# A retention head's values and normalised rows, transposed by DMA as two planes of 16-bit halves

## The chip, the cores and the metric

The kernel runs on one core of one Trainium2 chip. The time is device microseconds of one execution, the median of several runs; a profiled execution gives the trace. The engines are called as in the profile: PE (TensorE, its weight loads as PEld), DVE (VectorE), ACT (ScalarE), POOL (GpSimd), and SP, whose queue issues every DMA of this kernel.

## The reference

One layer of a decoder trunk: RMS norm, one input projection, two kinds of mixer side by side, an output projection, a residual and a last RMS norm. Sequence 2,048 (and 16 learned meta tokens ahead of it), width 1,024, all in float32.

```python
proj = einsum('bld,de->ble', rms_norm(h), w_in)          # 1024 -> 8 x 512
cx, cb, cc, cg, q, k, v, rg = split(proj, 8)
conv_out = short_conv(cx, cb, cc, conv_w) * silu(cg)     # 4 groups of 128
qf, kf = rotary(q) * 128**-0.5, rotary(k)                # 4 heads of 128
ret = retention_chunkwise(qf, kf, v)                     # chunks of 128, decay per head
y = (ret - mean(ret)) * rsqrt(var(ret) + eps)            # per head and row
ret_out = y * ret_norm_g * silu(rg)
out = rms_norm(h + concat(conv_out, ret_out) @ w_out) * final_g
```

Retention by chunks: `scores = (q k^T) * decay`, `out = scores v + q state`, and `state = decay * state + (k * zeta)^T v` from chunk to chunk.

## The kernel before

**Layout.** Sequence positions are handled in two halves of 1,024 (`r` = 0, 1; `NR`), each in two blocks of 512 columns (`j` = 0, 1; `HB`), each of four chunks of 128 (`c`; `CH`). A projection is computed with the 128 features of a head or group on the partitions and 512 positions in the free dimension.

**Quads.** Projections and the output projection are products of 2 x 2 blocks. `quad` (L203) does a 2 x 2 by 2 x 2 block product with seven products in place of eight (a Strassen-Winograd form), each product being 12 matmuls of 128 x 128 by 128 x 512: four slices of the contraction, with each operand split into a rounded high part and a low rest, and three of the four cross products. The line of all these matmuls is L212. A block's high part is made by a cast on ACT (`wh`, L101) and the rest by a subtraction on DVE (`wl`, L113). Both go through rings of three tiles (`RING`), so that ACT and DVE run at most three products ahead of PE. Sums of weight blocks are made on POOL (L110, L113) in raw tiles (`ra`, eight of them, `RAW`). Three times in a quad a PSUM bank is copied to SBUF by ACT (`copy`, L219), after the products numbered 0, 2 and 3. The function `take` handles each of the four results as it is done. `quad_plain` is the plain form with eight products, used at the start of each half.

**Units.** A half has eight units, in the order of `UNITS`: four `conv_group`s and four `head`s (in the first half a convolution group comes first, then heads 0 to 3; in the second, heads 0 to 3 and then the groups). A unit has two quads. Head `h` projects keys and values in the first quad and queries and gate in the second; `take` adds the bank copy to the bank (or copies the bank by ACT where there is nothing to add, L585), turns queries and keys (`rotary`), and applies SiLU to the gate (`sg`). Then, for each block `j`:

- four PE transposes of the keys (L631), scaled by `kd_col` on ACT (L633); four PE transposes of the values (L636), each chunk scaled by its rows' factors on ACT (L640, out of PSUM into the same tile);
- the chunks' state products (L646) and the chain of states (L649);
- scores (L659), masked and scaled (L661); output `o` from scores and state (L669, L670);
- mean and variance of each row (L675, L677), the power on POOL (L682), the normalised rows `y` on DVE (L686), in the tile `pm`;
- four PE transposes of `y` into a PSUM bank (L693); one DVE instruction multiplies this by the norm gain and the gate (L694); `store_mixed` (L444) writes the result to a DRAM tensor `mixed`, which the output projection reads at the end.

Between heads of the first half, `prepare` loads blocks of x (L361), makes their block sums on DVE and stores them (L190) for the second half; in the second half the same is done for the output weights.

**What sets the order.** The kernel is written as straight program text; a planner at build time simulates the engines' timelines and fixes for each engine, and for SP's queue, one order of instructions. At run time each engine works through its list in order and waits at an instruction until its inputs and buffers are there. So the retention of one head is laid between the next head's quads on PE. `tc.issue_after(ins)` puts the instructions in its block behind `ins` in the list of `ins`'s engine, and binds no other engine. Most working tiles (`kv`, `qg`, `x`, `t`, `w`, and so on) come from one pool of 16 tiles (`gen`, tag `g`, `GEN` = 16). SP issues, in its order, weight loads (L436), x loads, stores of sums and `mixed` stores.

Of the kernel before, what the change touches and what calls it, by code (L numbers as in the profile page):

```python
# [8 lines left out]
F32 = mybir.dt.float32  # L9
F32R = mybir.dt.float32r  # L10
BF16 = mybir.dt.bfloat16
AF = mybir.ActivationFunctionType
ALU = mybir.AluOpType

P = 128
# [6 lines left out]
HB = 512  # L22
NR = 2
BLK = SEQ // NR
CH = HB // P
KH = KT // 2
# [44 lines left out]
def hybrid_trunk(ctx: ExitStack, tc: tile.TileContext, t, out: bass.AP, chunk_decay):  # L71
# [5 lines left out]
    nc = tc.nc  # L77
# [11 lines left out]
    def ps_misc():  # L89
        return ps.tile([P, HB], F32, name="ms", tag="ms", bufs=4)  # L90

    def gen(name="g"):
        return sb.tile([P, HB + 16], F32, name=name, tag="g", bufs=GEN)[:, : 2 + HB]
# [29 lines left out]
    def stationary(blocks):  # L123

        a11, a12, a21, a22 = blocks
        s1 = sb.tile([P, HB], F32, name="sa", tag="ra", bufs=RAW)

        def parts(src):
            hi = sb.tile([P, HB], F32R, name="wh", tag="wh", bufs=RING)
            lo = sb.tile([P, HB], F32R, name="wl", tag="wl", bufs=RING)  # L130
            split(hi, lo, src)
            return hi, lo

        w = [parts(a11), parts(a12)]
        add(nc.gpsimd, s1, a21, a22)
        sub(nc.gpsimd, a21, a11, a21)
        sub(nc.gpsimd, a11, s1, a11)
        sub(nc.gpsimd, a12, a12, a11)
        return w + [parts(a) for a in (a11, s1, a21, a12, a22)]
# [53 lines left out]
    def prepared(m, src, ns, held={}):  # L193

        for n in ns:
            for kt in range(KH):
# [3 lines left out]
                    nc.sync.dma_start(a, src[n, kt])  # L200
                parts(m, SUMS[n], kt, a)

    def quad(w, m, take):  # L203


        def product(i, bank, first):
            (wh, wl) = w[i]
            for kt in range(KH):
                ks = slice(kt * P, (kt + 1) * P)
                mh, ml = m[i][kt]  # L210
                for n, (a, b) in enumerate(((wl, mh), (wh, ml), (wh, mh))):
                    nc.tensor.matmul(  # L212
                        bank, a[:, ks], b, start=first and kt == 0 and n == 0, stop=kt == KH - 1 and n == 2,
                        skip_group_check=not first,
                    )

        def copy(bank):
            c = sb.tile([P, HB], F32, name="tc", tag="tc", bufs=COPIES)
            nc.scalar.copy(out=c, in_=bank)  # L219
            return c  # L220

        xb = ps_proj()
        product(0, xb, True)
        c = copy(xb)
        yb = ps_proj()
        product(1, yb, True)
        take(0, 0, yb, c)
        product(2, xb, False)
        u2 = copy(xb)
        zb = ps_proj()  # L230
        product(3, zb, True)
        c = copy(zb)
        product(4, xb, False)
        take(1, 1, xb, c)
        product(5, zb, False)
        take(0, 1, zb, u2)
        product(6, xb, False)
        take(1, 0, xb, None)
# [61 lines left out]
    ident = const.tile([P, P], F32, name="ident")  # L300
# [5 lines left out]
    ret_g = const.tile([P, NG], F32, name="ret_g")  # L306
# [135 lines left out]
    def store_mixed(r, j, kt, m):  # L442
        d = mixed[2 * r + j]
        nc.sync.dma_start(  # L444
            d[:, :, kt // KH, :, kt % KH, :].rearrange("a i p c -> p a i c"),
            m.rearrange("p (a i c) -> p a i c", a=2, i=2),
        )
# [67 lines left out]
    def conv_group(g, r, m, f, blocks, ahead):  # L515

        u = [gen("u") for _ in range(2)]
        rr, rr2 = ([a[:, j * HB : (j + 1) * HB] for j in range(2)] for a in f[:2])
        held = [None]

        def mul(eng, out, a, b):
            eng.tensor_tensor(out=out, in0=a, in1=b, op=ALU.mult)  # L522

        def take(i, j, pp, c):
            s = u[j][:, 2:]
            if c is None:
                mul(nc.vector, s, pp, s)
            elif i == 1:
                add(nc.vector, c, pp, c)
                held[0] = c  # L530
            else:
                add(nc.vector, s, pp, c)
                mul(nc.vector, s, s, rr2[j])
                if j == 1:
                    mul(nc.gpsimd, s, s, held[0])

        blocks, meta = blocks
        quad(stationary(blocks), m, take)
        if meta:
            meta_carry(g, meta)  # L540
        carry(u, g, r)
        cs = [taps(u[j], g) for j in range(2)]

        def take(i, j, pp, c):
            if i == 0:
                add(nc.vector, c, pp, c)
                mul(nc.vector, c, c, rr[j])
                nc.scalar.activation(c, c, AF.Silu)  # L548
                mul(nc.gpsimd, cs[j], cs[j], rr[j])
                mul(nc.gpsimd, cs[j], cs[j], c)  # L550
                return
            if c is not None:
                add(nc.vector, c, pp, c)
                pp = c
            mul(nc.vector, cs[j], pp, cs[j])

        n = 2 * (NG + g) + 1
        quad(stationary(load_raw(w_loads(n))), m, take)
        blocks = ahead()
        for j in range(2):  # L560
            store_mixed(r, j, g, cs[j])
        return blocks
# [3 lines left out]
    def rotary(a, table):  # L566
# [5 lines left out]
        nc.vector.tensor_tensor(out=a, in0=a, in1=table[:, 0, :], op=ALU.mult)  # L572
        turned[0] = nc.vector.tensor_tensor(out=a, in0=a, in1=rot[:, :w], op=ALU.add)

    def head(h, r, m, rot_t, f, blocks, ahead, first=(), between=()):


        between = iter(between)
        k, v = [None, None], [None, None]
        tables = [rot_t[:, :, j * HB : (j + 1) * HB] for j in range(2)]  # L580

        def take(i, j, pp, c):
            d = gen("kv")[:, :HB]
            if c is None:
                nc.scalar.copy(out=d, in_=pp)  # L585
            else:
                add(nc.vector, d, pp, c)
            if i == 0:
                rotary(d, tables[j])
                k[j] = d  # L590
            else:
                v[j] = d

        if len(first) > 0:
            quad_plain(first[0], m, take)
        else:
            quad(stationary(blocks[0]), m, take)
        next(between, lambda: None)()
        q, sg = [None, None], [None, None]

# [24 lines left out]
        blocks = ahead()  # L625
        states = [state[h]]
        vt = []
        for j in range(2):
            tp = ps_misc()
            for c in range(CH):  # L630
                nc.tensor.transpose(tp[:, c * P : (c + 1) * P], k[j][:, c * P : (c + 1) * P], ident)  # L631
            kd = brief("kd")
            nc.scalar.mul(kd, tp, kd_col[:, h : h + 1])  # L633
            tp = ps_misc()
            for c in range(CH):
                nc.tensor.transpose(tp[:, c * P : (c + 1) * P], v[j][:, c * P : (c + 1) * P], ident)  # L636
            vj = v[j]
            for c in range(CH):
                cs = slice(c * P, (c + 1) * P)
                nc.scalar.mul(vj[:, cs], tp[:, cs], f[2][j][0][:, c : c + 1])  # L640
            vt.append(vj)
            last = r == NR - 1 and j == 1
            up = ps_misc()
            for c in range(CH - last):
                cs = slice(c * P, (c + 1) * P)
                nc.tensor.matmul(up[:, cs], kd[:, cs], vj[:, cs], start=True, stop=True)  # L646
            for c in range(CH - last):
                nxt = sb.tile([P, P], F32, name="state", tag="state", bufs=2 * CH)
                nc.vector.scalar_tensor_tensor(  # L649
                    out=nxt, in0=states[-1], scalar=chunk_decay[h], in1=up[:, c * P : (c + 1) * P],  # L650
                    op0=ALU.mult, op1=ALU.add,
                )
                states.append(nxt)

        for j in range(2):
            sc = ps_misc()
            for c in range(CH):
                cs = slice(c * P, (c + 1) * P)
# [3 lines left out]
                out=pm.rearrange("p (c i) -> p c i", c=CH), in0=sc.rearrange("p (c i) -> p c i", c=CH),  # L662
                scalar=past_col[:, h : h + 1],
                in1=causal.rearrange("p (c i) -> p c i", c=1).broadcast_to([P, CH, P]), op0=ALU.mult, op1=ALU.mult,
            )
            o = ps_misc()
            for c in range(CH):
                cs = slice(c * P, (c + 1) * P)
# [14 lines left out]
            y = pm  # L683
            for c in range(CH):
                cs = slice(c * P, (c + 1) * P)
                nc.vector.tensor_scalar(  # L686
                    out=y[:, cs], in0=o[:, cs], scalar1=mv[:, c, 0:1], scalar2=rp[:, c, :],
                    op0=ALU.subtract, op1=ALU.mult,
                )
            yT = ps_misc()  # L690
            for c in range(CH):
                cs = slice(c * P, (c + 1) * P)
                nc.tensor.transpose(yT[:, cs], y[:, cs], ident)  # L693
            nc.vector.scalar_tensor_tensor(  # L694
                out=sg[j], in0=yT, scalar=ret_g[:, h : h + 1], in1=sg[j], op0=ALU.mult, op1=ALU.mult
            )
            store_mixed(r, j, KH + h, sg[j])
        if r < NR - 1:
            nc.gpsimd.tensor_copy(out=state[h], in_=states[-1])
        return blocks  # L700
# [81 lines left out]
    for r in range(NR):  # L782
        f = factors[r]
# [120 lines left out]
```

## Time and profile before

| | |
|---|---|
| median of 3 runs | 894.16 us (893.94 to 894.59) |
| the profiled execution | 893.76 us, its span 892.0 us |
| granted TensorE clock, mean | 0.999 |
| busy PE / DVE / ACT / POOL | 879.8 / 717.7 / 407.2 / 397.8 us |
| DMA | 116.94 MB, 131 GB/s mean |

Busy times are unions of an engine's instructions; a matmul's recorded length overlaps the next one's, so what an instruction occupies is read from the distance between starts. The heads of the first half lie between about 64 and 295 us, those of the second between about 389 and 606 us. In groups and timelines, `out<-in` are the program's tile names, and `L212` is a line of the kernel.

### The profile page before, as it was taken

Reading aid. Unit: us, or ns where it says so; the run is one execution under the profiler, and the core shown is the slowest. Engines: PE = TensorE matmul, PEld = TensorE weight load, DVE = VectorE, ACT = ScalarE, POOL = GpSimd, SP = SyncE. Lnnn points to the kernel's source line nnn. Section 1 sums busy time; section 2 is a strip of 40 time slices with the busy share of each in tenths; the row PEclk is TensorE's granted clock in tenths of the full one; section 3 lists DMA queues with packets and bytes.
Section 4 is the critical chain, followed back from the end, with each engine's and each line's share of the span. In section 5 each row is a group of like instructions: output and inputs, shape, how many; then the busy total and the mean of one; then the engine's idle time right before and its main releaser. Section 6 shows DMA issues by size and latency. Waiting matters only on the chain.

```text
span 892.0 us, 12867 instructions
## 1 busy us (share of the span) xinstructions
PE 879.8 (99%) x4407; PEld 725.0 (81%) x4407; DVE 717.7 (80%) x1176; ACT 407.2 (46%) x816; POOL 397.8 (45%) x291
## 2 busy tenths in 40 slices
PE   8999999999999999999999999999999999999996
PEld 5778788888888778888888888888888888788885
DVE  6788887988967966999889899777668699766764
ACT  8674424234245364746243332423333476545553
POOL 0554222313134654452323323345546454787773
PEclk9999999999999999999999999999999999999999
DMA  9711224354224252834135272313131393555532
GB/s 336 231 65 48 72 54 150 129 159 149 73 83 142 83 154 75 293 117 141 48 95 200 71 245 87 96 58 95 49 93 49 117 390 101 183 165 160 183 121 81
DMA packets 76242, 116.94 MB, mean 131 GB/s; under 512 B 7632, under 2 KB 24336, under 8 KB 76176
## 3 DMA queue, kind: packets, MB, share of 16 engines
q1 hardware_dynamic: 76176, 116.11, 40.3%
q8 instruction: 35, 0.57, 0.3%
q14 instruction: 31, 0.25, 0.1%
HBM read 90.92 MB, written 25.17 MB: 130 GB/s over the span
## 4 chain that ended last, share of the span: by engine, by line
PE 82%; DVE 8%; DMA 4%; issue 2%; ACT 2%; POOL 2%; SPq 0%; POOLq 0%; DVEq 0%; ACTq 0%
PE pj L212 66%; PE pj L262 6%; DVE ml L113 2%; PE ms L669 1%; PE ms L670 1%; PE ms L659 1%; PE ms L646 1%; DMA w<-in_w_out 1%; DMA ra<-in_w_in 1%; PE ms L397 1%; DVE wl L113 1%; PE ms L693 1%; DVE ml L105 1%; PE ms L631 1%; PE ms L636 1%
## 5 line engine op out<-in xcount | busy, mean ns | idle before, releaser
L212 PE MATMUL pj<-mh,wl 128*128 128x512 f32 x1008 | 399.1, 396 | 1.5 <-ACT wh L101 0.6
L212 PE MATMUL pj<-ml,wh 128*128 128x512 f32 x1008 | 393.3, 390 | 0.0
L212 PE MATMUL pj<-mh,wh 128*128 128x512 f32 x1008 | 393.0, 390 | 0.0
L101 ACT CAST wh<-ra 128x512 fp32r<-128x512 f32 x216 | 134.0, 621 | 311.0 <-PE pj L212 264.9
L212 PEld LDWEIGHTS pj<-mh,wl 128*128 128x128 f32 x1008 | 189.4, 188 | 43.2 <-issue 2.2
L113 DVE TENSOR_TENSOR wl<-ra,wh 128x512 fp32r<-128x512 f32 x216 | 194.1, 899 | 34.5 <-ACT wh L101 34.0
L212 PEld LDWEIGHTS pj<-mh,wh 128*128 128x128 f32 x1008 | 189.2, 188 | 39.9
L212 PEld LDWEIGHTS pj<-ml,wh 128*128 128x128 f32 x1008 | 189.5, 188 | 37.8 <-issue 0.5
L113 POOL TENSOR_TENSOR ra<-ra 128x512 f32<-128x512 f32 x72 | 112.8, 1566 | 84.1 <-DVE qg L614 32.3
L110 POOL TENSOR_TENSOR sa<-ra 128x512 f32<-128x512 f32 x36 | 54.9, 1526 | 120.6 <-DVE wl L113 53.1
L113 POOL TENSOR_TENSOR ra<-sa,ra 128x512 f32<-128x512 f32 x36 | 52.0, 1444 | 92.6 <-DVE wl L113 89.1
L219 ACT COPY tc<-pj 128x512 f32<-128x512 f32 x108 | 62.7, 580 | 0.0
L262 PE MATMUL pj<-ml,mh 128*128 128x512 f32 x128 | 50.2, 392 | 0.1
L262 PE MATMUL pj<-mh,mh 128*128 128x512 f32 x128 | 49.9, 392 | 0.0
L262 PE MATMUL pj<-mh,ml 128*128 128x512 f32 x128 | 48.7, 397 | 0.7 <-DVE ml L113 0.6
L682 POOL TENSOR_TENSOR rp<-rs,neg_half 128x4 f32<-128x4 f32 x16 | 19.9, 1246 | 48.1 <-DVE rs L110 47.8
L723 DVE TENSOR_TENSOR yo<-pj,yo 128x512 f32<-128x512 f32 x32 | 21.9, 686 | 17.6 <-PE pj L212 7.8
L101 ACT CAST wh<-sa 128x512 fp32r<-128x512 f32 x36 | 22.4, 621 | 29.1 <-PE pj L212 28.9
L522 POOL TENSOR_TENSOR c<-c,rr 128x512 f32<-128x512 f32 x14 | 26.1, 1865 | 19.6 <-DVE c L459 9.6
L686 DVE TENSOR_SCALAR pm<-ms,mv,rp 128x128 f32<-128x128 f32 x64 | 21.9, 404 | 15.8 <-POOL rp L682 15.8
L522 POOL TENSOR_TENSOR c<-c,tc 128x512 f32<-128x512 f32 x14 | 26.1, 1862 | 18.7 <-ACT tc L548 18.7
L728 POOL TENSOR_TENSOR z<-yo,final_g 128x512 f32<-128x512 f32 x16 | 26.9, 1682 | 15.9 <-DVE yo L723 15.9
(137 smaller groups left out, 1145.5 us busy)
## 6 DMA issues: line engine op xcount, KB each, us to landing
ra<-in_w_in SPq DMA_DIRECT2D x128, 256.0 KB, 2.7
x<-in_xT SPq DMA_DIRECT2D x48, 256.0 KB, 4.8
w<-in_w_out SPq DMA_DIRECT2D x32, 256.0 KB, 5.2
ra<-mixed SPq DMA_DIRECT2D x32, 256.0 KB, 2.6
yo<-in_x SPq DMA_DIRECT2D x32, 256.0 KB, 4.5
ra<-in_x SPq DMA_DIRECT2D x16, 256.0 KB, 3.2
mixed<-c SPq DMA_DIRECT2D x16, 256.0 KB, 2.6
mixed<-qg SPq DMA_DIRECT2D x16, 256.0 KB, 2.3
```

The costliest lines, as they stand in the source:

```text
L101: nc.scalar.copy(out=hi, in_=src)
L105: nc.vector.scalar_tensor_tensor(out=lo, in0=src, scalar=scale, in1=hi.bitcast(F32), op0=ALU.mult, op1=ALU.subtract)
L110: eng.tensor_tensor(out=out, in0=a, in1=b, op=ALU.add)
L113: eng.tensor_tensor(out=out, in0=a, in1=b, op=ALU.subtract)
L212: nc.tensor.matmul(bank, a[:, ks], b, start=first and kt == 0 and n == 0, stop=kt == KH - 1 and n == 2, skip_group_check=not first,)
L219: nc.scalar.copy(out=c, in_=bank)
L262: nc.tensor.matmul(banks[i], a[:, ks], b, start=half + kt + n == 0, stop=half == 1 and kt == KH - 1 and n == 2,)
L522: eng.tensor_tensor(out=out, in0=a, in1=b, op=ALU.mult)
L682: nc.gpsimd.tensor_tensor(out=rp, in0=rs, in1=neg_half.rearrange("p (c a) -> p c a", a=1), op=ALU.pow)
L686: nc.vector.tensor_scalar(out=y[:, cs], in0=o[:, cs], scalar1=mv[:, c, 0:1], scalar2=rp[:, c, :], op0=ALU.subtract, op1=ALU.mult,)
L723: last[0] = nc.vector.tensor_tensor(out=y, in0=pp, in1=y, op=ALU.add)
L728: nc.gpsimd.tensor_tensor(out=ys[i][j], in0=y, in1=final_g[:, j * HB : (j + 1) * HB], op=ALU.mult)
```

## The change

The PE transposes of values (L636) and of normalised rows (L693) are replaced by transposes done by DMA. Such a DMA moves 16-bit elements, so a float32 tile of 512 columns is first written by ACT as two planes, all low halves and then all high halves (`turn`). One DMA of 256 KB, issued on SP, transposes the eight 128 x 128 blocks of the planes. ACT then puts the halves together again (`whole`).

- Values: `turn` is called in `take`, from the PSUM bank where there is no bank copy to add, else from the sum. `whole` and the scaling by row factors (from SBUF now, in place) are placed behind the last bank copy of the head's second quad, `copied[0]`.
- Normalised rows: `turn(y)` follows the normalisation. What comes after it (`whole`, the multiply by gain and gate, the store to `mixed`) is kept in a list, `pending`, and run by `catch_up` after the next unit's first quad, with ACT's part behind that quad's last bank copy.
- Each of the 32 halves takes three more tiles of the general pool: `pl`, `tr`, `wo`.

```diff
+    copied = [None]
...
         def copy(bank):
             c = sb.tile([P, HB], F32, name="tc", tag="tc", bufs=COPIES)
-            nc.scalar.copy(out=c, in_=bank)
+            copied[0] = nc.scalar.copy(out=c, in_=bank)
             return c
...
         quad(stationary(blocks), m, take)        # conv_group, first quad
+        catch_up()
...
+    def halves(a):
+        return a.bitcast(U16).rearrange("p (n two) -> p two n", two=2)
+
+    def planes(a):
+        return a.bitcast(U16).rearrange("p (two n) -> p two n", two=2)
+
+    def turn(a):
+        apart, across = gen("pl")[:, :HB], gen("tr")[:, :HB]
+        nc.scalar.copy(out=planes(apart), in_=halves(a))
+        nc.sync.dma_start(
+            across.bitcast(U16).rearrange("p (c f) -> p c f", c=2 * CH), apart.bitcast(U16), transpose=True
+        )
+        return across
+
+    def whole(across):
+        a = gen("wo")[:, :HB]
+        nc.scalar.copy(out=halves(a), in_=planes(across))
+        return a
+
+    pending = []
+
+    def catch_up():
+        if pending:
+            with tc.issue_after(copied[0].ins):
+                while pending:
+                    pending.pop(0)()
...
         def take(i, j, pp, c):                   # head, first quad
+            if i == 1 and c is None:
+                v[j] = turn(pp)
+                return
...
             else:
-                v[j] = d
+                v[j] = turn(d)
...
             quad(stationary(blocks[0]), m, take)
+            catch_up()
...
+        with tc.issue_after(copied[0].ins):      # head, after its second quad
+            for j in range(2):
+                v[j] = whole(v[j])
+                for c in range(CH):
+                    cs = slice(c * P, (c + 1) * P)
+                    nc.scalar.mul(v[j][:, cs], v[j][:, cs], f[2][j][0][:, c : c + 1])
         for j in range(2):
...
-            tp = ps_misc()
-            for c in range(CH):
-                nc.tensor.transpose(tp[:, c * P : (c + 1) * P], v[j][:, c * P : (c + 1) * P], ident)
             vj = v[j]
-            for c in range(CH):
-                cs = slice(c * P, (c + 1) * P)
-                nc.scalar.mul(vj[:, cs], tp[:, cs], f[2][j][0][:, c : c + 1])
...
-            yT = ps_misc()
-            for c in range(CH):
-                cs = slice(c * P, (c + 1) * P)
-                nc.tensor.transpose(yT[:, cs], y[:, cs], ident)
-            nc.vector.scalar_tensor_tensor(
-                out=sg[j], in0=yT, scalar=ret_g[:, h : h + 1], in1=sg[j], op0=ALU.mult, op1=ALU.mult
-            )
-            store_mixed(r, j, KH + h, sg[j])
+
+            def finish(j=j, across=turn(y)):
+                nc.vector.scalar_tensor_tensor(
+                    out=sg[j], in0=whole(across), scalar=ret_g[:, h : h + 1], in1=sg[j], op0=ALU.mult, op1=ALU.mult
+                )
+                store_mixed(r, j, KH + h, sg[j])
+
+            pending.append(finish)
```

More of the change, by code (lines that the diff above doesn't have):

```diff
@@ L11 @@
 BF16 = mybir.dt.bfloat16
+U16 = mybir.dt.uint16
 AF = mybir.ActivationFunctionType
```

## The prediction

> **What bounds the kernel now.** I read the page from its top: busy shares, the slices, the chain that ended last.
>
> ```profile
> span 892.0 us, 12867 instructions
> PE 879.8 (99%) x4407; PEld 725.0 (81%) x4407; DVE 717.7 (80%) x1176; ACT 407.2 (46%) x816; POOL 397.8 (45%) x291
> PEclk9999999999999999999999999999999999999999
> PE 82%; DVE 8%; DMA 4%; issue 2%; ACT 2%; POOL 2%; SPq 0%; POOLq 0%; DVEq 0%; ACTq 0%
> ```
>
> The span is 892.0 us, and PE is idle for 12.2 us of it, nearly all at the two ends. The granted clock is full in every slice, so nothing is to be had there. The chain is 82% PE. A PE instruction taken away should therefore shorten the span by the time it occupies in PE's stream, as long as nothing else is close behind.
>
> What is close behind is read from the table of stretches. Its columns are the length, then busy time and instruction count of PE, PEld, DVE, ACT and POOL, then the granted clock, the DMA share and GB/s. The first row is one head of the first half, the other three are heads of the second half.
>
> ```profile
> 148.00:198.00 50.00, 50.00 (x290) 42.05 (x290) 44.11 (x90) 18.87 (x40) 14.71 (x11) 1.00 0.40 132
> 425.00:470.00 45.00, 45.00 (x237) 38.36 (x236) 37.10 (x71) 16.11 (x32) 13.78 (x10) 1.00 0.28 83
> 470.00:512.00 42.00, 41.68 (x218) 35.11 (x217) 38.11 (x72) 13.22 (x25) 15.02 (x10) 1.00 0.40 131
> 512.00:560.00 48.00, 48.00 (x251) 40.89 (x250) 44.75 (x84) 15.47 (x31) 15.04 (x10) 1.00 0.49 156
> ```
>
> Inside the heads, the only place that the change touches, PE has no gap, but VectorE is busy for 37.10 to 44.75 us of 42 to 50. It has 3.25 us to spare in the tightest stretch (512 to 560). ScalarE has about 30 us to spare in each.
>
> **The change part by part.** *Removed from PE:* the four transposes of each value half (L636) and of each normalised half (L693). The groups view (count, busy us, mean ns of one, idle before) and PE's timeline (start, length, engine, line) show them.
>
> ```profile
> L693 PE MATMUL ms<-ident,pm 128*128 128x128 f32 x64 | 12.2, 274 | 0.3 <-DVE pm L686 0.3
> L636 PE MATMUL ms<-ident,kv 128*128 128x128 f32 x64 | 10.2, 273 | 0.0
> ```
>
> ```profile
> 190.86 0.39 PE L212 MATMUL pj<-mh,wh 128*128 128x512 f32 x1
> 191.10 0.60 PE L693 MATMUL ms<-ident,pm 128*128 128x128 f32 x4
> 191.45 0.48 PE L212 MATMUL pj<-mh,wl 128*128 128x512 f32 x1
> 191.76 0.40 PE L212 MATMUL pj<-ml,wh 128*128 128x512 f32 x1
> 192.00 0.40 PE L212 MATMUL pj<-mh,wh 128*128 128x512 f32 x1
> ...
> 156.46 0.60 PE L636 MATMUL ms<-ident,kv 128*128 128x128 f32 x4
> 156.82 0.48 PE L212 MATMUL pj<-mh,wl 128*128 128x512 f32 x1
> 157.13 0.40 PE L212 MATMUL pj<-ml,wh 128*128 128x512 f32 x1
> 157.37 0.39 PE L212 MATMUL pj<-mh,wh 128*128 128x512 f32 x1
> 157.60 0.39 PE L212 MATMUL pj<-mh,wl 128*128 128x512 f32 x1
> ```
>
> The 273 ns is one record's length; records overlap, so the price is read from starts. Undisturbed products start 0.23 us apart (157.37 to 157.60). From the product at 190.86 to the second one behind the group, at 191.76, pass 0.90 us where two steps would take 0.46: the group of four costs 0.44 us. The L636 group starts at 156.46 and gives way at 156.82, and the first step behind it is 0.31 instead of 0.23; that dearer first step stays, because other small products still precede it. So its price is 0.36 to 0.44. There are 64 / 4 = 16 groups of each kind: 16 x 0.44 + 16 x (0.36 to 0.44) = 12.8 to 14.1 us. I take 13.5 us, 1.7 us for each of the eight heads. Two turns of the miscellaneous PSUM banks per half go with them; that counts for nothing, since PE shows no gap in the heads that it could close.
>
> *Added on ScalarE:* for each of 32 halves a copy into planes and a copy back. An f32 row of 512 becomes 1,024 16-bit elements. Its nearest rows are ScalarE's copies out of PSUM; the second group is the plain copy of values and keys, part of which the copy into planes replaces.
>
> ```profile
> L219 ACT COPY tc<-pj 128x512 f32<-128x512 f32 x108 | 62.7, 580 | 0.0
> L585 ACT COPY kv<-pj 128x512 f32<-128x512 f32 x11 | 6.3, 586 | 21.6 <-PE pj L212 17.9 <-PE pj L262 3.6
> L425 ACT COPY state<-ms 128x128 f32<-128x128 f32 x4 | 1.0, 258 | 0.0
> ```
>
> (580 - 258) / 384 gives 0.84 ns an element, so 1,024 elements cost 0.58 + 512 x 0.84 ns = 1.01 us if the time goes by elements (0.58 if it goes by bytes, 2.0 if every other 16-bit element halves the rate). I take 1.01, since both rows follow elements. 64 copies are 65 us; 9 of the 11 L585 copies (7 heads with one value half, one with two) go, 5.3 us. Net +59 us, 7.4 a head, against a ScalarE that works 13 to 19 us of a head: busy time is no limit. The scaling of values by row factors (L640) stays, on another source, at the same price. The final multiply (L694) reads SBUF in place of PSUM; I take no difference.
>
> *Order on ScalarE.* This engine takes its work in order, and it also feeds PE with the rounded weights (wh). Its timeline in one head (idle time and releaser in brackets), and the group of VectorE's subtracts that follow the casts:
>
> ```profile
> 157.25 1.13 ACT L640 ACTIVATE kv<-ms,rc 128x128 f32<-128x128 f32 x4
> ...
> 174.50 0.59 ACT L585 COPY kv<-pj 128x512 f32<-128x512 f32 x1 [2.10 <-PE pj L212]
> ...
> 186.42 0.58 ACT L219 COPY tc<-pj 128x512 f32<-128x512 f32 x1
> 188.57 0.62 ACT L101 CAST wh<-ra 128x512 fp32r<-128x512 f32 x1 [1.57 <-PE pj L212]
> 189.10 0.58 ACT L219 COPY tc<-pj 128x512 f32<-128x512 f32 x1
> 191.29 0.62 ACT L101 CAST wh<-ra 128x512 fp32r<-128x512 f32 x1 [1.62 <-PE pj L212]
> ```
>
> ```profile
> L113 DVE TENSOR_TENSOR wl<-ra,wh 128x512 fp32r<-128x512 f32 x216 | 194.1, 899 | 34.5 <-ACT wh L101 34.0
> ```
>
> The last value half is copied out at 174.50. Its copy back may start behind the second quad's last bank copy, 189.10 + 0.58 = 189.68. The trip through the planes has 189.68 - 174.50 - 1.01 = 14.2 us. Behind the copies back then stand the next casts (191.29). A cast is released when PE leaves a ring slot, three deep, so PE needs it two products later. A product is 12 x 0.227 = 2.7 us, so it has 5.4 us, less cast (0.62) and the VectorE subtract behind it (0.90): 3.9 us at most, some 3.5 with a little queueing. Two copies back with eight scalings, 2 x 1.01 + 2 x 1.13 (four scalings, at 157.25), are 4.3 us if nothing is put between: a stall of under 1 us is possible. For the normalised rows the copy back isn't bound by its marker: y of one head is made while the next head's quads run (L693 at 191.10, in that next head's second quad), after the bank copy it is to stand behind. There the order rests on when the planner believes the transfer to land.
>
> *Added on the DMA queue:* 32 moves of 256 KB, all issued on SP, which also issues every weight load. No transposing transfer is in this trace, so its landing time D is bounded by the nearest rows (KB each, median us to landing; then packets, MB and share of 16 engines).
>
> ```profile
> mixed<-qg SPq DMA_DIRECT2D x16, 256.0 KB, 2.3
> x<-in_xT SPq DMA_DIRECT2D x48, 256.0 KB, 4.8
> rot_t<-in_rot SPq DMA_DIRECT2D x2, 1024.0 KB, 6.6
> q1 hardware_dynamic: 76176, 116.11, 40.3%
> ```
>
> Below: 2.3 us, the store that starts from SBUF. Above: 0.403 x 892 x 16 / 76,176 = 75 ns of an engine a packet; a block row of 128 16-bit elements is 256 bytes, so 1,024 packets, 75 ns each on 16 engines, 4.8 us; in runs of 64 bytes 19 us. I take 4.8, which the x loads also show. In either of the first two cases it ends well inside 14.2 us. The load on the engines is then 4 x 4.8 = 19 us a head beside 0.40 x 50 = 20 us of now: 39 of 48, so it fits.
>
> [...]
>
> *Queues.* SP: transposes wait for ScalarE's plane copy; what is queued behind them are weight loads, whose blocks have eight buffers, two quads (38 us) ahead, so a few us are covered. POOL gets nothing new. Buffers of the general tag (16): planes, transposed and whole copies add up to three per half, and the gate tile of a head lives on until the transposed rows are back, 1.01 + D + 1.01 = 7 us longer. Eight x tiles are fetched at one time in a head, beside eight tiles of the head itself, which is all 16:
>
> ```profile
> 192.73 0.38 SPq L444 DMA_DIRECT2D mixed<-qg  x1
> 193.16 3.84 SPq L361 DMA_DIRECT2D x<-in_xT  x8
> ```
>
> They follow directly on the release of the gate tile and will be up to 7 us late; what is late next is VectorE's block sums, work with no reader until the second half.
>
> *Sum against the profiled execution* (893.76 us, its span 892.0, so 1.76 around it; 0.4 below the median of the runs, 894.16): -13.5 for PE. Against it I set +2 us: about 0.25 us a head for casts late behind copies back or VectorE's tight stretch, between 0 and the whole 13.5, nearer the small end since ScalarE and the queue have room. On the median, 894.16 - 11.5 = 882.7.
>
> **The rivals.** (a) *VectorE becomes the bound.* PE's 48 us in the stretch from 512 becomes 46.3 with VectorE at 44.75, 97%; it also waits on POOL and ScalarE in order. For it: VectorE is already 91 to 93% busy where the chain leaves PE. Against: part of its work there (sums of the output weights) may move to looser stretches. Half the gain is left: about 888.
>
> (b) *The transposing transfers are slow and the queue becomes the bound; slower.* The place is SP's rings, in every head. If each transfer holds the rings for its whole landing time, it breaks even where 4 D + 20 us reaches the old 50 us of a head, D = 7.5 us; at D = 8.5 a head is 54 us, and 894 + 8 x 4 = 926; at D = 9, 942; from there up 32 us more with each us of D. For it: 16-bit pieces, never seen in this trace. Against: the x loads' 4.8 us.
>
> (c) *A new in-order wait on ScalarE; slower.* A copy back of y reaches the head of ScalarE's queue before its transfer has landed, and the cast behind it is more than 3.5 us late. A wait of 4.5 us costs PE 1 us; on all 32 copies +32, at half of them +16: 894 - 13.5 + 16 = 897, to 912. It decides once the copies back cost PE 0.42 us each on average (13.5 / 32).
>
> (d) *It cancels out,* within 0.2%.
>
> **How the numbers follow.** Chances: forecast (877 to 886) 0.45; (a) 0.20; (d) 0.08; (c) 0.17; (b) 0.10. Faster or slower counts beyond 0.2%, 1.8 us, about what a measurement of this kernel can tell. Faster 0.45 + 0.19 = 0.64, with 0.01 of (a) falling to same; same 0.09; slower 0.27. The likeliest case's own range is 877 to 886. The full one reaches from 877 to 905, which leaves out (b) and the dear half of (c), together under 0.2.
>
> **What would show it.** The L636 and L693 groups gone; PE's products in a head still 0.23 us apart and the head 1.7 us shorter; ScalarE's groups of copies near 1.0 us and its busy time near 465; transposes landing in under 7 us. Wrong: casts or copies on ScalarE that wait for DMA, PE idle behind wh or wl, a DMA share near 1 in the heads, weight loads that POOL or ScalarE waits for.

## The result, and the profile after

The changed kernel takes 952.91 us (951.44 to 954.49, four runs) against 894.36 for the kernel before: the ratio is 1.0653, 95% interval 1.0638 to 1.0668. It is slower by 58.6 us. The forecast was 882.7, with 905 as the upper end of the range.

The page of the changed kernel (line numbers are about three higher near the quad and up to 38 higher behind the head; L212 is L215 now, L110 is L111, L686 is L724):

```profile
span 951.9 us, 12712 instructions
PE 880.9 (93%) x4279; PEld 720.6 (76%) x4279; DVE 699.1 (73%) x1176; ACT 472.8 (50%) x871; POOL 390.1 (41%) x291
PEclk9999999989799999999989989799999999999999
q1 hardware_dynamic: 109968, 124.50, 42.4%
```

The 128 transposes are gone (4,407 PE instructions became 4,279), yet PE's busy time didn't fall, and PE is now idle for 951.9 - 880.9 = 71.0 us instead of 12.2. The granted clock has dips that it didn't have (0.970 on the mean instead of 0.999). The DMA share hardly rose (40.3% before). PE's groups (count, busy us, mean ns, then idle time before and what ended it) name the wait:

```profile
L215 PE MATMUL pj<-mh,wl 128*128 128x512 f32 x1008 | 403.7, 401 | 58.4 <-DVE kv L111 51.1 <-ACT tc L222 3.6 <-DVE tc L111 1.3
```

Of the 58.4 us, 51.1 end with one kind of instruction: VectorE's addition that makes a key or value half out of a PSUM bank and its copy (`kv<-pj,tc`), in the first quad of a head. There are six such waits, one at each passage from a head to the next (three in each half), 4.54 to 11.69 us long. The first of them, in PE's timeline:

```profile
128.32 0.39 PE L708 MATMUL ms<-state,qg 128*128 128x128 f32 x2
133.24 0.79 PE L215 MATMUL pj<-mh,wl 128*128 128x512 f32 x1 [4.54 <-DVE kv L111]
133.83 0.63 PE L215 MATMUL pj<-ml,wh 128*128 128x512 f32 x1
134.26 0.63 PE L215 MATMUL pj<-mh,wh 128*128 128x512 f32 x1
...
135.97 0.63 PE L215 MATMUL pj<-mh,wl 128*128 128x512 f32 x1
136.39 0.45 PE L215 MATMUL pj<-ml,wh 128*128 128x512 f32 x1
...
136.92 0.40 PE L215 MATMUL pj<-mh,wl 128*128 128x512 f32 x1
137.15 0.40 PE L215 MATMUL pj<-ml,wh 128*128 128x512 f32 x1
```

PE stops behind the last product of the old head's output (L708), since the PSUM banks of the next head's first quad have not been emptied. After the 4.54 us of idling its products come 0.43 us apart (133.83 to 134.26) instead of 0.23 (136.92 to 137.15), until 136.4; the granted clock is 0.50 there. So each wait costs twice: the idle time, and behind it 3.2 to 5.3 us of products at the low clock.

What VectorE does in that time, in the changed kernel and, below it, in the kernel before:

```profile
123.76 1.36 DVE L724 TENSOR_SCALAR pm<-ms,mv,rp 128x128 f32<-128x128 f32 x4 [1.13 <-POOL rp L720]
...
128.74 0.89 DVE L713 BATCH_NORM_STATS2 st<-ms 128x6 f32<-128x128 f32 x4 [0.39 <-PE ms L708]
...
131.23 1.36 DVE L724 TENSOR_SCALAR pm<-ms,mv,rp 128x128 f32<-128x128 f32 x4 [1.12 <-POOL rp L720]
132.51 1.28 DVE L111 TENSOR_TENSOR kv<-pj,tc 128x512 f32<-128x512 f32 x2
```

```profile
106.98 0.67 DVE L110 TENSOR_TENSOR kv<-pj,tc 128x512 f32<-128x512 f32 x1
...
116.95 0.69 DVE L110 TENSOR_TENSOR kv<-pj,tc 128x512 f32<-128x512 f32 x1 [0.47 <-PE pj L212]
...
121.17 1.37 DVE L686 TENSOR_SCALAR pm<-ms,mv,rp 128x128 f32<-128x128 f32 x4 [1.13 <-POOL rp L682]
122.46 0.68 DVE L110 TENSOR_TENSOR kv<-pj,tc 128x512 f32<-128x512 f32 x1
...
123.77 0.69 DVE L570 TENSOR_TENSOR rot<-kv,rot_t 64x512 f32<-64x512 f32 x1
...
137.77 1.37 DVE L686 TENSOR_SCALAR pm<-ms,mv,rp 128x128 f32<-128x128 f32 x4 [0.91 <-POOL rp L682]
```

Before, two of the next head's three additions (106.98 and 116.95) ran ahead of the old head's first normalisation, and the third (122.46) between the two, 15 us ahead of the second (137.77). After, both blocks of the old head are normalised first (123.76 and 131.23), and the additions follow directly on the second one, at 132.51, two in a row. It is so at all six passages: in the changed kernel none of the additions stands ahead of the second normalisation, in the kernel before at least one of them stands ahead even of the first. Nothing in these rows waits for a transfer. The additions show no wait of their own; VectorE's list has them in another order.

The added work itself does what it was to do. ScalarE's groups of copies and the transfers (issue length min/median/max, then landing):

```profile
L597 ACT COPY wo<-tr 128x1024 uint16<-128x1024 uint16 x32 | 41.6, 1357 | 0.0
L589 ACT COPY pl<-pm 128x1024 uint16<-128x1024 uint16 x16 | 16.7, 1046 | 23.1 <-DVE pm L724 23.1
L589 ACT COPY pl<-pj 128x1024 uint16<-128x1024 uint16 x9 | 9.1, 1012 | 14.9 <-PE pj L215 14.8
```

```profile
L590 SPq DMA_TRANSPOSE tr<-pl x32: 1232/1238/1934, 75.3 to 657.7; - x32
DMA to landing us min/median/max: 2.7/3.1/5.0
```

A transfer lands in 3.1 us and holds SP for 1.24; no copy back in this kernel waits for one (idle 0.0). A plain weight load, from SP's timeline, holds it for a quarter of that:

```profile
128.42 0.33 SPq L439 DMA_DIRECT2D ra<-in_w_in  x1
```

### The profile page after: what moved, and what is told of

It reads as the page before. It is cut to its first block, busy times and chain, and to the rows that moved or that the text cites. A ratio compares the mean times of both kernels' runs of the same rounds, so it can differ in the third digit from the quotient of the medians.

```text
span 951.9 us, 12712 instructions
## 1 busy us (share of the span) xinstructions
PE 880.9 (93%) x4279; PEld 720.6 (76%) x4279; DVE 699.1 (73%) x1176; ACT 472.8 (50%) x871; POOL 390.1 (41%) x291
## 3 DMA queue, kind: packets, MB, share of 16 engines
q1 hardware_dynamic: 109968, 124.50, 42.4%
## 5 line engine op out<-in xcount | busy, mean ns | idle before, releaser
L215 PE MATMUL pj<-mh,wl 128*128 128x512 f32 x1008 | 403.7, 401 | 58.4 <-DVE kv L111 51.1
L215 PE MATMUL pj<-ml,wh 128*128 128x512 f32 x1008 | 397.6, 394 | 1.1 <-DVE ml L114 1.1
L215 PE MATMUL pj<-mh,wh 128*128 128x512 f32 x1008 | 397.4, 394 | 0.0
L215 PEld LDWEIGHTS pj<-mh,wl 128*128 128x128 f32 x1008 | 192.3, 191 | 106.7 <-DVE kv L111 52.7
L114 DVE TENSOR_TENSOR wl<-ra,wh 128x512 fp32r<-128x512 f32 x216 | 183.0, 849 | 81.9 <-ACT wh L102 81.2
L215 PEld LDWEIGHTS pj<-ml,wh 128*128 128x128 f32 x1008 | 192.5, 191 | 40.7 <-DVE ml L114 1.6
L215 PEld LDWEIGHTS pj<-mh,wh 128*128 128x128 f32 x1008 | 192.0, 190 | 40.9
L114 POOL TENSOR_TENSOR ra<-ra 128x512 f32<-128x512 f32 x72 | 106.4, 1478 | 96.3 <-PE ms L400 58.0
L111 POOL TENSOR_TENSOR sa<-ra 128x512 f32<-128x512 f32 x36 | 54.8, 1523 | 134.4 <-DVE wl L114 76.2
L597 ACT COPY wo<-tr 128x1024 uint16<-128x1024 uint16 x32 | 41.6, 1357 | 0.0
L763 ACT ACTIVATE rot<-yo 128x512 f32<-128x512 f32 x32 | 20.1, 630 | 32.1 <-DVE yo L761 31.7
L761 DVE TENSOR_TENSOR yo<-pj,yo 128x512 f32<-128x512 f32 x32 | 21.9, 686 | 19.2 <-POOL yo L111 12.2
L724 DVE TENSOR_SCALAR pm<-ms,mv,rp 128x128 f32<-128x128 f32 x64 | 21.9, 403 | 18.0 <-POOL rp L720 18.0
```

The costliest lines, as they stand in the source:

```text
L111: eng.tensor_tensor(out=out, in0=a, in1=b, op=ALU.add)
L114: eng.tensor_tensor(out=out, in0=a, in1=b, op=ALU.subtract)
L215: nc.tensor.matmul(bank, a[:, ks], b, start=first and kt == 0 and n == 0, stop=kt == KH - 1 and n == 2, skip_group_check=not first,)
L597: nc.scalar.copy(out=halves(a), in_=planes(across))
L724: nc.vector.tensor_scalar(out=y[:, cs], in0=o[:, cs], scalar1=mv[:, c, 0:1], scalar2=rp[:, c, :], op0=ALU.subtract, op1=ALU.mult,)
L761: last[0] = nc.vector.tensor_tensor(out=y, in0=pp, in1=y, op=ALU.add)
```

## The experiments

Theory A: a tile of the general pool is handed out in the order in which the program asks for it. The changed kernel asks for the tiles of the normalised rows (`pl`, `tr`) ahead of the next head's key and value tiles in the program's text, so the planner can't place the key additions until the normalisation has its tiles. Theory B: the added copies and transfers, each in order on its queue, cost the time. Theory C: the pool has too few tiles. The three differ in what they say of versions that change the request alone, the number alone, or the transfers alone. Each ratio below is to the kernel before, run beside the version (medians of 894.0 to 894.6 us).

**One request alone.** The kernel before, with the normalised rows written into a fresh tile of the pool:

```diff
-            y = pm
+            y = gen("y")[:, :HB]
```

> The kernel before, with one edit: the normalised rows are written into a tile asked of the general pool instead of over the score tile. No copy, no transfer, no instruction is added; PE transposes as before. Theory A: the next head's key and value additions wait behind the normalised rows, with PE idle 5 to 12 us in most heads and the low clock behind it: 930 to 970 us. Theory B: 894, as before. Theory C: nearly as before, 894 to 905, since two tiles more are asked for in a head.

Measured 951.05 us (950.69 to 951.38), ratio 1.0634 (1.0618 to 1.065), against 894 by B and at most 905 by C: a loss of 56.8 us, about as large as the changed kernel's net loss, with no copy, no transfer and no instruction added. (The changed kernel also has 13 us less PE work, so its loss before that saving is some 72 us; the request alone isn't all of that.) Its PE groups and VectorE's timeline:

```profile
L212 PE MATMUL pj<-mh,wl 128*128 128x512 f32 x1008 | 403.0, 400 | 24.9 <-DVE kv L110 17.9 <-ACT tc L219 3.1 <-DVE wl L113 2.8
L693 PE MATMUL ms<-ident,y 128*128 128x128 f32 x64 | 16.4, 320 | 12.7 <-DVE y L686 12.7
```

```profile
131.31 1.37 DVE L686 TENSOR_SCALAR y<-ms,mv,rp 128x128 f32<-128x128 f32 x4 [1.12 <-POOL rp L682]
132.59 1.87 DVE L110 TENSOR_TENSOR kv<-pj,tc 128x512 f32<-128x512 f32 x3
```

Again the key and value additions stand directly behind the second normalisation, here three in a row, and PE waits for them, or, where its transposes come first, for the rows themselves (12.7 us). The second normalisation itself waits 1.12 us, for the power on POOL, about as in the kernel before (0.91): the row shows no wait for its own tile.

**The control.** The same, with the rows written into the key tile, which is done with by then (`y = k[j]`).

> The control to that: the kernel before, with the normalised rows written into the key tile, which is done with by then. Same instructions, no request. All theories: 894 us within 0.5%.

Measured 894.64 us, ratio 1.0003 (0.9994 to 1.0013). A tile that exists already costs nothing; that one is asked for does.

**The number of tiles.** The kernel before with `GEN` = 12 instead of 16.

> The kernel before with 12 tiles in the general pool instead of 16. Theory A: the order of requests is the old one, so no long wait for key and value additions; at most a few us for loads that start later, 894 to 905 us. Theory C: four tiles are as many as the changed kernel holds for its normalised rows, so a loss like its own, 930 or more. Theory B says nothing here.

Measured 907.01 us (901.95 to 909.79), ratio 1.0136 (1.0101 to 1.017). Four tiles fewer cost 12.7 us, a little over what A allowed; C's 930 isn't reached. So the number of tiles isn't free, but it doesn't bring this loss. A larger pool with the request in place was not run. PE's wait for key additions is small here:

```profile
L212 PE MATMUL pj<-mh,wl 128*128 128x512 f32 x1008 | 398.3, 395 | 3.2 <-DVE kv L110 2.2 <-ACT wh L101 0.7 <-DVE wl L113 0.3
```

**The place of the request.** The changed kernel with its 16 tiles; `turn(y)` is called behind the next unit's first quad, and the rest behind its second.

```diff
-            def finish(j=j, across=turn(y)):
+            def begin_turn(j=j, y=y):
+                across = turn(y)
+                def finish():
...
+                finishing.append(finish)
-            pending.append(finish)
+            pending.append(begin_turn)
```

> The pool and its 16 tiles as in the changed kernel; only the place of the request is moved: the planes of the normalised rows are asked for and written behind the next unit's first quad, and the copy back stands behind its second quad. Tiles are held longer than in the changed kernel. Theory A: 880 to 900 us. Theory B: 940 or more. Theory C: 952 or more, since gate tiles are held for a quad longer.

Measured 906.42 us (904.89 to 908.52), ratio 1.0134 (1.0113 to 1.0155). Every copy and transfer is there, tiles are held longer, and 46 of the 58 us are back. At every passage a key or value addition again stands ahead of the old head's first normalisation. It is 6 us above the end of A's range: PE's largest wait is now for the weights' low parts (`wl`), 10.2 us.

**Tiles of their own.** `GEN` = 13, and three tiles under a tag of their own for the planes of the normalised rows; copies back go into the tile of the planes.

```diff
-RING, RAW, GEN, COPIES = 3, 8, 16, 4
+RING, RAW, GEN, COPIES = 3, 8, 13, 4
...
+    def own():
+        return sb.tile([P, HB], F32, name="ow", tag="ow", bufs=3)
...
-            def finish(j=j, across=turn(y)):
+            def finish(j=j, across=turn(y, own(), own())):
```

> The pool is cut to 13 tiles and three tiles of their own are given to the planes and transposed planes of the normalised rows; in all 16 as in the changed kernel, and every copy and transfer as there, all copies back into the tile of the planes. Theory A: the additions no longer wait, 880 to 895 us. Theory B: 940 or more. Theory C: with three tiles fewer for all else and no tile more in all, no better than 952.

Measured 923.09 us (918.44 to 924.77), ratio 1.031 (1.0278 to 1.0342). Between A's range and B's. PE's largest waits here are for bank copies on ScalarE (`tc`, 16.5 us) and `wl` (6.0), none for key additions. ScalarE waits 35.9 us there at copies back for their transfers, which can hold the bank copies up; the pool of 13 may cost by itself too, as the pool of 12 did, but wasn't run alone. It speaks against C, not more.

**Parts alone.** Only the rows, or only the values, by DMA, each with its tiles from the pool.

> Only the normalised rows go by DMA, with their tiles asked of the general pool as in the changed kernel; the values are transposed on PE as before. Theory A: all the waits of the changed kernel stay, half of PE's saving goes: 950 to 970 us. Theory B: half of the loss, 915 to 930.

> Only the values are transposed by DMA; the normalised rows are transposed on PE as before. Theory A: no request stands between two heads any more, so no wait, and half of the PE saving: about 894 - 6.5 = 886 to 890 us. Theory B: half of the loss stays, 915 to 930. Theory C: most of the pool's pressure stays (three tiles a half), above 900.

Rows alone: 939.91 us, ratio 1.0508 (1.0491 to 1.0526), PE waiting 31.2 us for key additions. Values alone: 897.48, ratio 1.004 (1.0025 to 1.0054). The rows' part carries nearly all of the loss, as A says, though 10 us less than it said. The values don't hold the next head up, but bring nothing either: A's 886 to 890 is missed.

**The whole change without a request for the rows.** Planes into the query tile, transposed planes into the key tile (both free by then), copies back into the tile of the planes:

```diff
-    def turn(a):
-        apart, across = gen("pl")[:, :HB], gen("tr")[:, :HB]
+    def turn(a, apart=None, across=None):
+        if apart is None:
+            apart, across = gen("pl")[:, :HB], gen("tr")[:, :HB]
...
-            def finish(j=j, across=turn(y)):
+            def finish(j=j, across=turn(y, q[j], k[j])):
```

> All 64 ScalarE copies and 32 transposing transfers stay, but no tile of the general pool is asked for between one head's normalised rows and the next head's keys: the planes of the rows go into the query tile, the transposed planes into the key tile, and the copy back into the tile of the planes. Theory A (a request for a tile of the general pool is served in program order, so the next head's key and value tiles wait until the last head's normalised rows have theirs): PE's waits for the key and value additions, 51.1 us in all, go, the low clock behind them goes, and the transposes' 13.5 us show: 878 to 886 us. Theory B (the added copies and transfers, in order on ScalarE and SP, cost the time): 940 us or more. Theory C (too few tiles in the pool): also 878 to 890, since this version asks for fewer.

Measured 895.18 us (892.94 to 898.64), ratio 1.0009 (0.9995 to 1.0023). All of the loss is gone, with all 64 copies and 32 transfers in place: B falls. But the 13.5 us of saved PE work don't show, and A's 878 to 886 (and C's 878 to 890) are missed. VectorE's order is the old one again, the key addition between the normalisations:

```profile
121.62 1.37 DVE L725 TENSOR_SCALAR pm<-ms,mv,rp 128x128 f32<-128x128 f32 x4 [1.13 <-POOL rp L721]
122.90 0.68 DVE L111 TENSOR_TENSOR kv<-pj,tc 128x512 f32<-128x512 f32 x1
...
131.96 1.36 DVE L725 TENSOR_SCALAR pm<-ms,mv,rp 128x128 f32<-128x128 f32 x4 [0.90 <-POOL rp L721]
```

The groups of this version:

```profile
L215 PE MATMUL pj<-mh,wl 128*128 128x512 f32 x1008 | 399.2, 396 | 9.0 <-ACT tc L222 7.8 <-DVE wl L114 0.7 <-DVE kv L111 0.3
L708 PE MATMUL ms<-pl,pm 128*128 128x128 f32 x128 | 25.1, 277 | 2.3 <-DVE pm L700 2.3
L598 ACT COPY qg<-kv 128x1024 uint16<-128x1024 uint16 x16 | 21.7, 1355 | 24.0 <-DMA kv<-qg 24.0
```

and two of its heads (columns as in the prediction's table):

```profile
148.00:198.00 50.00, 48.92 (x276) 40.31 (x276) 44.77 (x91) 27.68 (x49) 20.53 (x12) 1.00 0.52 158
198.00:249.00 51.00, 49.68 (x280) 40.91 (x279) 45.84 (x92) 28.49 (x50) 21.67 (x12) 1.00 0.40 117
```

ScalarE now waits 24.0 us for transfers at its copies back (theory D: this takes the gain), and VectorE is as busy as before in heads that should be shorter, with PE waiting for masked scores (theory E: VectorE's room takes it).

**Where the gain went.** Four versions: the copy back of the rows on GpSimd; values alone with copies back in place; and the kernel before and the reusing version, both with the VectorE instructions of the block sums between heads left out.

```diff
-                    out=sg[j], in0=whole(across), ...
+                    out=sg[j], in0=whole(across, nc.gpsimd.tensor_copy), ...     # reuse_pool
...
         if f is not None:
             nc.scalar.mul(b11, b11, f)
+        if leave:                                                               # the two without sums
+            return
```

> As the version that reuses the query and key tiles (895.2 us), but the copy back of the normalised rows runs on GpSimd instead of ScalarE. In that version ScalarE waits 24.0 us in all, in 15 of 16 cases, at such a copy for its transfer, and PE waits 7.8 us for bank copies behind it. Theory D (the in-order wait on ScalarE takes the gain): those waits go, 884 to 888 us. Theory E (VectorE has no room in the heads of the first half, 44.8 to 45.8 us busy of 50 to 51, and PE now waits for its masked scores): no change beyond 2 us, 893 to 896. Under both, slower if GpSimd's 16-bit copies delay its block sums.

> Only the values by DMA, with the copy back into the tile of the planes, so one tile less is asked for per half than in the values-only version (897.5 us). The normalised rows on PE. Theory D: no copy back waits for a transfer here, the half saving shows: 887 to 889. Theory E: VectorE holds the heads where they are: 892 to 896. If the third tile of each half was what cost the values-only version its time, this one lies under it by that.

> The kernel before without the 32 VectorE instructions of the block sums that are prepared between heads (they are left out, so later products use unsummed blocks); VectorE is freed of about 23 us in six heads, PE's work is the same. PE had no gap in the heads: all theories 892 to 895 us.

> The version that reuses the query and key tiles, with the same 32 VectorE instructions left out. Theory E: with VectorE's room the transposes' saving shows in the six heads, 880 to 886 us, 8 to 13 below the kernel before with the same work left out. Theory D: ScalarE's waits are as long as before, so it stays within 3 us of it, 891 to 895.

On GpSimd: 894.37, ratio 0.9998 (0.9989 to 1.0008); D alone isn't it. Values in place: 891.72 (891.34 to 893.81), ratio 0.9976 (0.9966 to 0.9986): between D's range and E's, and faster than the kernel before by 0.24%, 2.3 us, where its 64 transposes were priced at 5.8 to 7.0 us; the tile asked for less per half is worth 5.8 us against the values-only version. The kernel before without sums: 893.45, ratio 0.9991 (0.9982 to 1.0). The reusing version without them: 887.03, ratio 0.9924 (0.9908 to 0.994). The same relief is worth 0.6 us before and 8.2 in the reusing version, and 6.4 of 13.5 us show with it, about half. That fits E, whose range ended at 886, but doesn't prove it: without the sums the prepared x tiles also go back to the pool sooner (their first store is issued at 144.5 us instead of 151.7), and these runs don't separate that from VectorE's room. In the two pages, the kernel before without sums and then the reusing version without them, PE's busy time stands for the saved work itself:

```profile
PE 879.5 (99%) x4407; PEld 725.0 (81%) x4407; DVE 695.8 (78%) x1144; ACT 407.5 (46%) x816; POOL 397.2 (45%) x291
```

```profile
PE 866.6 (98%) x4279; PEld 710.6 (80%) x4279; DVE 700.8 (79%) x1144; ACT 472.2 (53%) x871; POOL 395.9 (45%) x291
```

879.5 - 866.6 = 12.9 us at the same clock (0.999): the price of the 128 transposes, forecast at 12.8 to 14.1.

**Both reliefs, and another place for the sums.**

> Reused tiles, the block sums prepared between heads left out, and the copy back of the normalised rows on GpSimd, so that ScalarE waits for no transfer. If VectorE's room and ScalarE's in-order waits together take the saving: 880 to 883 us, against 887.0 with the waits. If ScalarE's waits cost nothing on PE: 886 to 888.

> The control: the kernel before with the block sums in the same new place. PE had no gap in the heads: 892 to 895 us.

> Reused tiles, all work done; the block sums prepared for later stand between the convolution groups (two steps after each of two of them) instead of behind heads. If the sums' place in the heads costs what leaving them out gave: 886 to 889 us. If VectorE's total work is what counts: 893 to 896.

> Only the values by DMA, copied back in place, rows on PE (891.7 us), with the block sums in the new place. If VectorE's room in the heads is what that version lacked: 887 to 889; otherwise 891 to 893.

Reused tiles without sums, with the copy back on GpSimd: 885.92 (885.63 to 886.41), ratio 0.9904 (0.989 to 0.9919); 1.1 us below the one without GpSimd, so ScalarE's waits cost little, not the 4 to 7 us of the first expectation. PE still waits 2.8 us there for bank copies on ScalarE; the rest of the way to 880 isn't explained. The sums between the convolution groups: 903.22 for the kernel before (1.0097, 1.0082 to 1.0112), 898.94 for the reusing version (1.005, 1.0035 to 1.0065), 897.85 for values alone (1.0032, 1.0022 to 1.0042). The control came out unlike its expectation: the new place costs the kernel before 8.7 us by itself, so these three don't tell whether the place or the sums count. Against that control the reusing version is 4.3 us and values alone 5.4 us faster.

## Why the prediction was wrong

**PE's saving: right.** 13.5 us forecast, 12.9 measured as PE's busy time on the same clock.

**The copies and the transfers: nearly right in size.** The copy into planes takes 1.01 to 1.05 us (1.01 taken), the copy back 1.36 (mis-sized by a third). A transfer lands in 3.1 us (4.8 taken), so rival (b), the slow queue, is out: 4 x 3.1 + 20 us are well under a head, and the DMA share rose only from 40.3% to 42.4%. The 3.1 us lies between the two rows of the kernel before that the prediction bounded it by: 2.3 for the plain store from SBUF, 4.8 for the x loads.

**The step that failed is the one on buffers.** The prediction counted the tiles of the general tag (three per half, a gate tile 7 us longer, x tiles up to 7 us late) and let VectorE's sums, "work with no reader until the second half", be what is late next; so it put the whole cost of the new requests at nothing. It asked how many tiles there are, not in which order they are asked for. One request between two heads puts the next head's key additions behind the normalised rows on VectorE; PE's banks stay full; PE idles 4.54 us in the wait shown, 51.1 in the six. The gate tile's longer life was mis-sized as well: from normalisation to gate multiply pass 20.5 and 13.0 us at the first passage, 7.0 and 3.8 before, so 9.2 and 13.5 us more and not 7. No rival named the wait. The nearest, (c), had the right shape, an in-order wait that holds PE up, but on ScalarE and for a transfer; in the changed kernel no copy back waits for one.

**The sum of what happened,** between the two spans: PE's saved work, -13.2 (879.8 to 866.6, the same products at full clock); the same work recorded longer, +14.3 (880.9 - 866.6), of which about 12 us are the products at the low clock behind the six waits, by the distances of their starts; idle time, +58.8 (71.0 - 12.2). Together +59.9 us, the difference of the spans (951.9 - 892.0). The prediction had no term for the clock, since there were no gaps to bring it down; each of the six waits brought one along.

**Rival (a) may have been real, but under the loss.** With the requests for the rows gone, nothing of the gain is left (895), where (a) left half (888). With VectorE's sums left out half of it shows (887); that this lies near (a)'s 888 is luck, since (a) spoke of a kernel with its sums. The +2 us against the gain were too few in either case: at 91% and more of a stretch, VectorE deserved more than a rival's 0.20.

**What is shown and what isn't.** That a request gives the loss is shown from both sides: put into the kernel before it costs 56.8 us, and with the rows' requests taken out of the changed kernel 57.7 us come back (952.9 to 895.2), all copies and transfers in place. Four tiles fewer cost 12.7 us, so the number alone doesn't give it. That the planner hands tiles out in program order is the reading that fits the orders on VectorE and the late request; the planner itself wasn't measured. Why the reusing version keeps nothing of the 13 us is shown in part only: leaving the sums out brings 8.2 us back, by VectorE's room or by the tiles they hold; GpSimd's copies bring about 1, and about 5 us are unaccounted for.

## What to carry to other kernels

Where a planner hands out tiles of a shared pool, price a new tile by what stands behind its request in the program: if the next stage asks from the same pool, it may be chained (by the reading that fits these runs) to the moment when your tile is first written. Write into a tile that is done with, or ask later, before you buy any bandwidth. And take work off the busiest engine only after a look at the second: PE's 1.5% didn't show here while VectorE was some 90% busy in the heads (44.77 of 50 us, 45.84 of 51).

## What the hardware showed

A PE pause of 4.54 us was followed by 3.2 us of products at nearly half the pace (0.43 us instead of 0.23, granted clock 0.50); behind pauses of 11.55 and 11.69 us it was 3.6 and 5.3 us. In the changed kernel this added about 12 us to 58.8 us of idling. In the reusing version, where PE's longest wait for a bank copy was 2.5 us, the granted clock was 0.96 in the stretch from 470 to 512 us and 1.00 in the other heads. ScalarE's copy of 1,024 16-bit elements costs 1.01 (from PSUM) to 1.05 us (from SBUF) when it gathers every other element to planes, and 1.36 us when it spreads planes back. A 256 KB transposing transfer from SBUF to SBUF landed in 3.1 us (2.7 to 5.0), where a plain store of that size took 2.3 in the kernel before and 2.8 in this one, but held SP for 1.24 us where a plain load held it for 0.33.
